# Expert products as three narrow products into one accumulator, values in one pass

## The chip, the cores and the metric

The kernel runs on one core of a Trainium2 chip. The metric is device time of one launch in microseconds (us). Engines are named as in the profile: PE is TensorE (PEld its weight loads), DVE is VectorE, ACT is ScalarE, POOL is GpSimd, SP is SyncE, which here only issues DMAs.

## The reference

One inference step of a transformer layer for 256 prompt tokens and 32 sample tokens, 288 in all, with 2048 columns each, in fp32. Cut to what matters:

```python
qkv   = x @ w_in                                   # differential attention, memory attention
x1    = layer_norm(ALPHA * x + mixed @ w_o)
q     = x1 @ peer_w_q                              # 8 heads x 2 keys x 128
s     = einsum('thcd,hcnd->thcn', q, sub_keys)     # product keys: 16 best of 128 x 128 experts per head
act   = einsum('td,tkd->tk', x1, u_tab[experts])   # 128 experts per token, 16384 in all
h     = gelu(act) * gates
y     = layer_norm(ALPHA * x1 + einsum('tk,tkd->td', h, v_tab[experts]))
```

The change concerns the last lines: the activations `act` and the values `y`.

## The kernel before

The tokens are split. For 224 "dense" tokens (`ND`) the kernel computes the activations of all 16,384 experts and masks them with the gates (zero where an expert was not chosen), so both expert tables are read once from HBM in order and are multiplied on TensorE. For the other 64 tokens the rows of the chosen experts are gathered by indirect DMAs on POOL's queue and are multiplied on VectorE.

fp32 accuracy comes from splitting: every number is hi + lo, each part in the 12 bits that one pass of TensorE carries (type fp32r). A product of weights w and data x is hi(w) hi(x) + hi(w) lo(x) + lo(w) hi(x).

**The stream.** `plan` lists all large loads in order, in units of 128 x 1024 numbers (512 KB). `stream`, `load_next` and `take` (lines 149 to 204) run it: SP's queue loads a unit into a ring of four `raw` tiles (L191), ScalarE casts it to `hi` (L165), VectorE subtracts to get `lo` (L181), and `hi` and `lo` are rings of three. `take` returns a unit's parts and at the same time issues the split of the unit two ahead and the load of the one four ahead. `tick` advances work that stands beside the stream by one stage. The order of all instructions is as written by hand; each engine works through its own queue in order.

**Activations** (lines 1031 to 1073). For each of 128 blocks of 128 experts two units of `peer_u`, transposed, give 16 steps, one for each contraction tile of 128. The moving data `ux` hold the hi part of 224 tokens and behind it their lo part, 448 columns. A step is one product of 448 columns (weights hi, L1039) and one of 224 columns (weights lo, L1041), which adds into the accumulator's first 224 columns. An accumulator is one PSUM bank. When a block is done, `finish_act` has ScalarE copy the second 224 columns into `small` (L992), multiplies them with an identity matrix into the first 224 columns (L994) and applies the gelu a stage later. In the second half of the blocks, one-hot products for the gates (L1019, four in a unit) stand in between.

**Values** (lines 1078 to 1272). The weights are the rows of `peer_v`, 128 experts x 1024 columns in a unit, and the moving data are h, hi and lo side by side, split in batches of four blocks (`batch`, L75 and L76). Eight accumulators of 448 columns fill the eight PSUM banks, so the 2048 output columns take two passes over the 128 expert blocks, one for each half of the columns, and h is split in both. A step is one 128 x 128 tile of weights: L1200 (448 columns) and L1202 (224 columns). At the end of a pass `evac` again copies the second half on ScalarE (L1117), adds it through the identity matrix (L1119), and VectorE adds the accumulator to the residual in `yT` (L1120). In the last units `turn` transposes the finished columns for the norm behind it (L1190). The gathered tokens' value rows (L948, L1111) are paced by the unit's number.

Each product on TensorE is issued with its own weight load. This is the step as the activation stage has it:

```python
nc.tensor.matmul(ps[:, :2 * ND], wh, ux[:, d].rearrange("p a t -> p (a t)"), start=(d == 0), stop=False, ...)
nc.tensor.matmul(ps[:, :ND], wl, ux[:, d, 0], start=False, stop=False, skip_group_check=True)
```

The projections of the earlier stages (`mm_tile`, L232 to L234) have three products of 256 or 288 columns for the same sum.

Of the kernel before, what the change touches and what calls it, by code (L numbers as in the profile page):

```python
# [10 lines left out]
F32R = mybir.dt.float32r  # L11
# [6 lines left out]
P = 128  # L18
D = 2048
DT = 16  # L20
# [17 lines left out]
LAG = 1  # L38
XCOLS = 928
# [10 lines left out]
def tile_stream_step(ctx: ExitStack, tc, xT_d, xn_d, memT_d, ckT_d, cv_d, cmkT_d, cmv_d,  # L50
# [22 lines left out]
    def split_to(hi, lo, raw):  # L73
        """raw = hi + lo exactly, each part in the 12 bits that one pass of the tensor engine carries"""
        nc.scalar.copy(hi, raw)  # L75
        nc.vector.tensor_sub(lo, raw, hi.bitcast(F32))  # L76

    # x1 rows of the gathered tokens, and the expert choices
# [26 lines left out]
    # ------------------------------------------------ the stream of everything large  # L105
# [38 lines left out]
    plan += [weight(v_d[i * P:(i + 1) * P, half * 1024:(half + 1) * 1024]) for half in range(2) for i in range(NKEY)]  # L144
# [4 lines left out]
    def stream(n, ahead=AHEAD):  # L149
        """splits up to the weights that are ahead units after unit n, and loads beyond them"""  # L150
# [26 lines left out]
    def settle():  # L177
        """the small parts that are due"""
        while pending:
            _, hi, lo, raw = pending.pop(0)  # L180
            nc.vector.tensor_sub(lo, raw, hi.bitcast(F32))  # L181
# [24 lines left out]
    # ------------------------------------------------ work beside the stream  # L206
    stages = []          # each advances by one stage per tick
    slow = deque()       # one at a time, by its cost on the vector engine
# [20 lines left out]
    def mm_tile(ps, part, k, d, mh, ml, n):  # L229
        """out^T [128 columns, n tokens] += one contraction tile of weights' (mh + ml)"""  # L230
        wh, wl = (w[:, k * P:(k + 1) * P] for w in part)
        nc.tensor.matmul(ps[:, :n], wh, mh[:, d, :n], start=(d == 0), stop=False)  # L232
        nc.tensor.matmul(ps[:, :n], wh, ml[:, d, :n], start=False, stop=False)  # L233
        nc.tensor.matmul(ps[:, :n], wl, mh[:, d, :n], start=False, stop=(d == DT - 1))  # L234

    def mm_unit(ps, half, mh, ml, n, ticks=(3, 7), tiles=8):
        """the next unit's contraction tiles"""
# [6 lines left out]
    def keep_warm(n):  # L244
        """products into a bank that nobody reads, so that the tensor engine's clock stays up over a pause"""
# [10 lines left out]
    def rsqrt(pool, out, v, n, rows=P):  # L256
        """out = (v + eps) ** -0.5, with a Newton step behind the square root's table"""
# [9 lines left out]
    # ------------------------------------------------ constants, memory projections  # L267
# [24 lines left out]
    def bias_job():  # L292
        """the relative bias of all heads, laid out by diagonals through DRAM"""
# [35 lines left out]
    # ------------------------------------------------ mixers  # L329
# [45 lines left out]
    def diff_attend(h, qT, kT, vT, ck, cv):  # L375
# [51 lines left out]
        def weights(t):  # L427
            # w * s0 = e0 - lam * s0 / s1 * e1
# [155 lines left out]
    # ------------------------------------------------ output projection, first norm  # L584
# [27 lines left out]
    def residual(c, ps):  # L612
        """the tokens' rows again, added to the residual"""
# [48 lines left out]
    # ------------------------------------------------ expert choice  # L662
    ROWS = (P, 96, P)

    def topk(units):
        """the 16 best experts of heads for the tokens of their tiles: scores, and both halves of their numbers;
        the units' steps take turns"""
# [89 lines left out]
    def dense_choice(t):  # L757
        """the choices of a dense token tile, its heads' units done"""
# [26 lines left out]
    def rows_job():  # L785
        """x1 rows of the gathered tokens"""
# [8 lines left out]
    def copy_job():  # L795
        """the dense tokens' part of x1, both parts side by side"""
# [13 lines left out]
    def normed_turn(c):  # L810
        """a tile of the normed rows, transposed"""
# [103 lines left out]
    # the last scores, before the units of the experts  # L915
# [8 lines left out]
    # ------------------------------------------------ experts: activations and gates  # L924
# [12 lines left out]
    class Rows:  # L937
        """half rows of the gathered tokens' experts, fetched ahead of their use"""
# [27 lines left out]
    def one_hots(t0):  # L966
        """of two tokens: the second key's choices, and the gates at the first key's"""
# [10 lines left out]
    def gate_in(t0, ps, done):  # L978
        """gates of four tokens for all experts: into h where the activation is there, aside elsewhere"""
# [9 lines left out]
    def finish_act(i, ps, gated):  # L989
        """the smaller products onto the others, and the activation; h where the gates are there"""  # L990
        small = tmpp.tile([P, ND], F32R, tag="small", name=f"small{i}")
        nc.scalar.copy(small, ps[:, ND:2 * ND])  # L992
        yield
        nc.tensor.matmul(ps[:, :ND], identr, small, start=False, stop=True, skip_group_check=True)  # L994
# [36 lines left out]
    for i in range(NKEY):  # L1031
        ps = pa()
        for half in range(2):
            n = 2 * i + half
            hi, lo = take()
            for k in range(8):
                d = half * 8 + k
                wh, wl = hi[:, k * P:(k + 1) * P], lo[:, k * P:(k + 1) * P]
                nc.tensor.matmul(ps[:, :2 * ND], wh, ux[:, d].rearrange("p a t -> p (a t)"), start=(d == 0), stop=False,  # L1039
                                 skip_group_check=True)  # L1040
                nc.tensor.matmul(ps[:, :ND], wl, ux[:, d, 0], start=False, stop=False, skip_group_check=True)  # L1041
# [36 lines left out]
    # ------------------------------------------------ experts: values  # L1078
# [4 lines left out]
    def batch(b, pieces=((0, 4),)):  # L1083
        if b < 64:
            i = 4 * (b % 32)
# [27 lines left out]
    def evac(half, dt, acc):  # L1113
        """the smaller products onto the others, and the sum onto the residual"""
        d = half * 8 + dt
        small = tmpp.tile([P, ND], F32R, tag="small", name=f"vsm{d}")
        nc.scalar.copy(small, acc[:, ND:2 * ND])  # L1117
        yield
        nc.tensor.matmul(acc[:, :ND], identr, small, start=False, stop=True, skip_group_check=True)  # L1119
        nc.vector.scalar_tensor_tensor(yT[:, d], yT[:, d], ALPHA, acc[:, :ND], op0=OP.mult, op1=OP.add)  # L1120
# [16 lines left out]
    def finish_gathered():  # L1137
        """the gathered tokens' halves together, their second norm, out"""
# [32 lines left out]
        # the rows of the dense tokens' norm, into what is free now  # L1171
# [13 lines left out]
    def turn(g, t):  # L1185
        """rows of a quarter of the columns again, in a free bank"""
# [8 lines left out]
    EARLY = {3: [(0, 0)], 4: [(1, 0), (0, 1)], 5: [(1, 1)], 6: [(2, 0)]}  # L1195
    def products(half, dt, part, i):
        """columns of the values (hi + lo) . a block's h, whole and remainder"""
        hb = batches[(half * NKEY + i) // 4][:, i % 4] if half or i else h0
        wh, wl = (w[:, dt * P:(dt + 1) * P] for w in part)
        nc.tensor.matmul(accs[dt][:, :2 * ND], wh, hb.rearrange("p a t -> p (a t)"), start=(i == 0), stop=False,  # L1200
                         skip_group_check=True)
        nc.tensor.matmul(accs[dt][:, :ND], wl, hb[:, 0], start=False, stop=False, skip_group_check=True)  # L1202

    evs, accs = [], []

    def finish(half, dt):
        """a finished accumulator's evacuation, begun; the one before it, ended"""
        g = evac(half, dt, accs[dt])
        next(g)
        if dt:  # L1210
            drain(evs.pop())
        evs.append(g)
        if half == 1:
            for g, t in EARLY.get(dt, ()):
                turn(g, t)
                quarter_stats(g, t)

    for half in range(2):
        tail = 2 + half
        groups = [[i] for i in range(NKEY - tail)] + [list(range(NKEY - tail, NKEY))]  # L1220
        for group in groups:
            last_group = len(group) > 1
            units = []
            for q, i in enumerate(group):
                units.append(take(AHEAD - q))
            if last_group and half == 1:
                while slow:
                    drain(slow.popleft())
            if group[0] == 0:
                accs[:] = [None] * 8  # L1230
            for dt in range(8):
                if group[0] == 0:
                    if half and dt == 2:
                        drain(evs.pop())
                    if not half and dt in (2, 4):
                        tick()
                    accs[dt] = pb() if dt < 4 else pa()
                for j, (part, i) in enumerate(zip(units, group)):
                    if j < 2:
                        products(half, dt, part, i)  # L1240
                    elif dt >= LAG:
                        products(half, dt - LAG, part, i)
                if len(group) == 2:
                    finish(half, dt)
                elif len(group) == 3 and dt >= LAG:
                    finish(half, dt - LAG)
            if len(group) == 3:
                for dt in range(8 - LAG, 8):
                    products(half, dt, units[2], group[2])
                    finish(half, dt)  # L1250
            if last_group and half == 1:
                turn(2, 1)
                drain(evs.pop())
                for t in range(2):
                    turn(3, t)
            n = half * NKEY + group[-1]
# [136 lines left out]
```

## Time and profile before

| | |
|---|---|
| median of 3 runs | 2013.01 us (2010.47 to 2014.66) |
| profiled execution, span | 2008.1 us (the profile gives no other time for it; 4.9 us under the median) |
| PE busy | 1983.6 us (99%), 13178 products |
| PEld busy | 1872.5 us (93%), 13178 loads |
| DVE busy | 1567.3 us (78%) |
| ACT busy | 1160.7 us (58%) |
| POOL busy | 480.9 us (24%) |
| DMA | 521.21 MB, mean 260 GB/s |
| mean granted TensorE clock | 0.997 |

The activation stage takes the span from 624.6 to about 1336 us, the value stage from there to about 1990 us. In the profile a product's duration includes its way through the array, and the ends are modelled, so neighbouring products overlap in it; the distance between two starts is what a product costs in a stream.

### The profile page before, as it was taken

To read this page: it belongs to the slowest core of one execution; us is meant where nothing else is said; L and a number is where in the kernel's file an instruction comes from. 1 tells how busy PE (TensorE), PEld (TensorE's weight loads), DVE (VectorE), ACT (ScalarE), POOL (GpSimd) and SP (SyncE) were. 2 spreads that over 40 slices of the span, in tenths; PEclk is the share of its full clock that TensorE was granted. 3 is DMA by queue.
4 is the path that set the end of the run, shared out by engine and by line. 5 is a ranking of instruction groups with operands and counts; after the bars stand their busy time and mean duration, and the time that the engine had idled before them with its cause. 6 is when DMAs were issued, how large, how long until landed. Compare 5 with 4: busy or idle time off the path is not lost.

```text
span 2008.1 us, 34989 instructions
## 1 busy us (share of the span) xinstructions
PE 1983.6 (99%) x13178; PEld 1872.5 (93%) x13178; DVE 1567.3 (78%) x2683; ACT 1160.7 (58%) x1919; POOL 480.9 (24%) x348
## 2 busy tenths in 40 slices
PE   9999999999999999999999999999999999999996
PEld 7999999999999999999999999999999999999996
DVE  5455555556788889998899999978888888888886
ACT  5345545544534555555999999854455555444553
POOL 0110000010000112222333333324443343334412
PEclk9999999999999999999999999999999999999998
DMA  8854555484445788888888888889999998999985
GB/s 294 258 165 141 153 155 153 129 287 137 154 148 162 241 291 280 277 282 283 294 298 296 293 298 302 300 288 318 335 322 343 327 333 314 323 328 321 327 264 167
DMA packets 147625, 521.21 MB, mean 260 GB/s; under 512 B 16848, under 2 KB 21088, under 8 KB 147328
## 3 DMA queue, kind: packets, MB, share of 16 engines
q1 hardware_dynamic: 103504, 360.49, 54.8%
q0 software_dynamic: 43952, 158.48, 22.0%
q8 instruction: 104, 1.70, 0.3%
q14 instruction: 65, 0.53, 0.1%
HBM read 508.33 MB, written 10.06 MB: 258 GB/s over the span
## 4 chain that ended last, share of the span: by engine, by line
PE 96%; DMA 1%; DVE 1%; ACT 1%; POOL 0%; issue 0%; SPq 0%; POOLq 0%; ACTq 0%; DVEq 0%
PE pa L1039 22%; PE pa L1200 11%; PE pb L1200 11%; PE pa L1041 11%; PE pa L232 8%; PE pa L233 7%; PE pa L234 7%; PE pb L1202 5%; PE pa L1202 5%; PE pb L1019 3%; DMA raw<-in_wmk 1%; PE pa L994 1%; PE pb L397 0%; DVE lo L181 0%; PE pa L893 0%; PE pa L319 0%
## 5 line engine op out<-in xcount | busy, mean ns | idle before, releaser
L181 DVE TENSOR_TENSOR lo<-raw,hi 128x1024 fp32r<-128x1024 f32 (+1 forms) x679 | 820.8, 1211 | 367.1 <-ACT hi L165 356.7
L165 ACT CAST hi<-raw 128x1024 fp32r<-128x1024 f32 (+1 forms) x679 | 705.5, 1040 | 497.2 <-PE pa L1200 253.8
L1039 PE MATMUL pa<-ux,hi 128*128 128x448 f32 x2048 | 669.8, 379 | 0.0
L1041 PE MATMUL pa<-ux,lo 128*128 128x224 f32 x2048 | 543.6, 265 | 0.0
L1039 PEld LDWEIGHTS pa<-ux,hi 128*128 128x128 f32 x2048 | 385.4, 188 | 29.4 <-issue 0.2
L1041 PEld LDWEIGHTS pa<-ux,lo 128*128 128x128 f32 x2048 | 391.7, 191 | 0.0
L948 POOL DMA_INDIRECT ur<-in_u,gidx x128 | 197.9, 1546 | 700.2 <-DVE ur L963 329.8
L1200 PE MATMUL pa<-hs,hi 128*128 128x448 f32 x1020 | 338.3, 376 | 0.0
L1200 PE MATMUL pb<-hs,hi 128*128 128x448 f32 x1020 | 338.0, 376 | 0.0
L948 POOL DMA_INDIRECT vr<-in_v,gidx x128 | 221.4, 1730 | 354.7 <-DVE x1g L1111 321.2
L1202 PE MATMUL pb<-hs,lo 128*128 128x224 f32 x1020 | 271.1, 266 | 0.3 <-DVE lo L181 0.3
L1202 PE MATMUL pa<-hs,lo 128*128 128x224 f32 x1020 | 271.0, 266 | 0.0
L1200 PEld LDWEIGHTS pb<-hs,hi 128*128 128x128 f32 x1020 | 191.4, 188 | 17.5
L1200 PEld LDWEIGHTS pa<-hs,hi 128*128 128x128 f32 x1020 | 191.4, 188 | 17.4
L1202 PEld LDWEIGHTS pb<-hs,lo 128*128 128x128 f32 x1020 | 195.1, 191 | 0.5 <-DVE lo L181 0.5
L232 PE MATMUL pa<-xh,hi 128*128 128x288 f32 x640 | 195.2, 305 | 0.0
L1202 PEld LDWEIGHTS pa<-hs,lo 128*128 128x128 f32 x1020 | 195.1, 191 | 0.0
L233 PE MATMUL pa<-xl,hi 128*128 128x288 f32 x640 | 188.9, 295 | 0.0
L234 PE MATMUL pa<-xh,lo 128*128 128x288 f32 x640 | 188.2, 294 | 0.0
L1111 DVE SCALAR_TENSOR_TENSOR x1g<-vr,ggate,x1g 128x1024 f32<-128x1024 f32 x128 | 163.7, 1279 | 0.0
L963 DVE SCALAR_TENSOR_TENSOR ur<-ur,x1g 128x1024 f32<-128x1024 f32 x128 | 155.7, 1216 | 0.0
L232 PEld LDWEIGHTS pa<-xh,hi 128*128 128x128 f32 x640 | 120.0, 188 | 4.9 <-issue 3.7
(346 smaller groups left out, 2706.7 us busy)
## 6 DMA issues: line engine op xcount, KB each, us to landing
raw<-in_ut SPq DMA_DIRECT2D x256, 512.0 KB, 4.4
raw<-in_v SPq DMA_DIRECT2D x255, 512.0 KB, 6.5
raw<-in_win SPq DMA_DIRECT2D x80, 512.0 KB, 3.7
raw<-in_wq SPq DMA_DIRECT2D x32, 512.0 KB, 3.6
raw<-in_wo SPq DMA_DIRECT2D x29, 512.0 KB, 3.7
raw<-in_wmv SPq DMA_DIRECT2D x8, 512.0 KB, 5.3
raw<-in_wmk SPq DMA_DIRECT2D x6, 512.0 KB, 5.8
xn<-in_xn POOLq DMA_DIRECT2D x8, 384.0 KB, 9.7
```

The source lines that it names most:

```text
L165: nc.scalar.copy(hi[:, cs], raw[:, cs])
L181: nc.vector.tensor_sub(lo, raw, hi.bitcast(F32))
L232: nc.tensor.matmul(ps[:, :n], wh, mh[:, d, :n], start=(d == 0), stop=False)
L233: nc.tensor.matmul(ps[:, :n], wh, ml[:, d, :n], start=False, stop=False)
L234: nc.tensor.matmul(ps[:, :n], wl, mh[:, d, :n], start=False, stop=(d == DT - 1))
L948: nc.gpsimd.indirect_dma_start(out=t, out_offset=None, in_=self.table, in_offset=bass.IndirectOffsetOnAxis(ap=gidx[:, a, s:s + 1], axis=0))
L963: nc.vector.scalar_tensor_tensor(rows, rows, 1.0, x1g[:, a * 1024:(a + 1) * 1024], op0=OP.mult, op1=OP.mult, accum_out=gact[:, a, s:s + 1])
L1039: nc.tensor.matmul(ps[:, :2 * ND], wh, ux[:, d].rearrange("p a t -> p (a t)"), start=(d == 0), stop=False, skip_group_check=True)
L1041: nc.tensor.matmul(ps[:, :ND], wl, ux[:, d, 0], start=False, stop=False, skip_group_check=True)
L1111: nc.vector.scalar_tensor_tensor(va, rows, ggate[:, s:s + 1], va, op0=OP.mult, op1=OP.add)
L1200: nc.tensor.matmul(accs[dt][:, :2 * ND], wh, hb.rearrange("p a t -> p (a t)"), start=(i == 0), stop=False, skip_group_check=True)
L1202: nc.tensor.matmul(accs[dt][:, :ND], wl, hb[:, 0], start=False, stop=False, skip_group_check=True)
```

## The change

A step has three products of 224 columns, all into the same 224 columns: hi(w) hi(x), hi(w) lo(x), lo(w) hi(x). The copies to `small`, the identity products and their stages in `finish_act` and `evac` are gone. In the value stage an accumulator now has 224 columns, two of them share a PSUM bank (`place`), and 16 accumulators hold all 2048 output columns, so there is one pass over the expert blocks: both column halves of a block follow each other (`V_ORDER`), h is split once (32 batches instead of 64), and all evacuations stand at the end. The last three blocks (`TAIL`) are ordered by halves, so that the first half's accumulators end early.

```diff
+    V_ORDER = [(i, half) for i in range(NKEY - TAIL) for half in range(2)]
+    V_ORDER += [(i, half) for half in range(2) for i in range(NKEY - TAIL, NKEY)]
+    plan += [weight(v_d[i * P:(i + 1) * P, half * 1024:(half + 1) * 1024]) for i, half in V_ORDER]
...
     def finish_act(i, ps, gated):
-        small = tmpp.tile([P, ND], F32R, tag="small", name=f"small{i}")
-        nc.scalar.copy(small, ps[:, ND:2 * ND])
-        yield
-        nc.tensor.matmul(ps[:, :ND], identr, small, start=False, stop=True, skip_group_check=True)
         yield
...
-                nc.tensor.matmul(ps[:, :2 * ND], wh, ux[:, d].rearrange("p a t -> p (a t)"), start=(d == 0), stop=False,
-                                 skip_group_check=True)
-                nc.tensor.matmul(ps[:, :ND], wl, ux[:, d, 0], start=False, stop=False, skip_group_check=True)
+                nc.tensor.matmul(ps[:, :ND], wh, ux[:, d, 0], start=(d == 0), stop=False, skip_group_check=True)
+                nc.tensor.matmul(ps[:, :ND], wh, ux[:, d, 1], start=False, stop=False, skip_group_check=True)
+                nc.tensor.matmul(ps[:, :ND], wl, ux[:, d, 0], start=False, stop=(d == DT - 1), skip_group_check=True)
...
+    def evac(d, n=1):
+        bank, at_ = place(d)
+        nc.vector.scalar_tensor_tensor(yT[:, d:d + n], yT[:, d:d + n], ALPHA,
+                                       banks[bank][:, at_ * ND:(at_ + n) * ND].rearrange("p (a t) -> p a t", a=n),
+                                       op0=OP.mult, op1=OP.add)
...
+    EARLY = {1: [(0, 0)], 2: [(0, 1)], 3: [(1, 0)], 4: [(1, 1)], 5: [(2, 0)], 6: [(2, 1)]}
+    def place(d):
+        return (d // 2, d % 2) if d < 8 else (4 + d % 4, (d - 8) // 4)
+
+    def products(d, part, i):
+        bank, at_ = place(d)
+        if bank not in banks:
+            banks[bank] = pb() if bank < 4 else pa()
+            first = True
+        else:
+            first = False
+        acc = banks[bank][:, at_ * ND:(at_ + 1) * ND]
+        hb = batches[i // 4][:, i % 4] if i else h0
+        wh, wl = (w[:, d % 8 * P:(d % 8 + 1) * P] for w in part)
+        nc.tensor.matmul(acc, wh, hb[:, 0], start=first, stop=False, skip_group_check=True)
+        nc.tensor.matmul(acc, wh, hb[:, 1], start=False, stop=False, skip_group_check=True)
+        nc.tensor.matmul(acc, wl, hb[:, 0], start=False, stop=(i == NKEY - 1), skip_group_check=True)
...
+    for n, (i, half) in enumerate(V_ORDER[:-TAIL]):
+        part = take()
+        for dt in range(8):
+            if n == 0 and dt in (2, 4):
+                tick()
+            products(half * 8 + dt, part, i)
+            if i == NKEY - 1 and dt % 2:
+                evac(dt - 1, 2)
+        beside(n)
+        if half == 0 and i % 4 == 1:
+            batch(i // 4 + 1)
+        if half == 1 and i % 4 == 3:
+            del batches[i // 4]
+    units = [take(AHEAD - q) for q in range(TAIL)]
...
+    for dt in range(8 + LAG):
+        for j, i in enumerate(range(NKEY - TAIL, NKEY)):
+            at_dt = dt - LAG if j == TAIL - 1 else dt
+            if 0 <= at_dt < 8:
+                products(8 + at_dt, units[j], i)
+        if dt >= LAG:
+            evac(8 + dt - LAG)
+            for g, t in EARLY.get(dt - LAG, ()):
+                turn(g, t)
+                quarter_stats(g, t)
```

## Rows read from the trace of the kernel before

**Rows 1.** Windows: start:end, length, busy us (count) by engine, clock, DMA share, GB/s.
```profile
624.00:800.00 176.00, 176.00 (x1129) 167.06 (x1128) 154.88 (x385) 98.92 (x147) 27.99 (x19) 1.00 0.78 257
1220.00:1300.00 80.00, 80.00 (x543) 76.53 (x542) 74.94 (x143) 72.67 (x166) 29.71 (x19) 1.00 0.84 294
1400.00:1500.00 100.00, 100.00 (x633) 94.62 (x632) 84.37 (x73) 50.33 (x50) 41.08 (x26) 1.00 0.94 329
```

**Rows 2.** Part 4 of the page: the chain that ended last, by engine.
```profile
PE 96%; DMA 1%; DVE 1%; ACT 1%; POOL 0%; issue 0%; SPq 0%; POOLq 0%; ACTq 0%; DVEq 0%
```

**Rows 3.** Groups, PE, value stage: shapes xcount, busy us, mean ns, idle us.
```profile
L1202 PE MATMUL pb<-hs,lo 128*128 128x224 f32 x1020 | 271.1, 266 | 0.3 <-DVE lo L181 0.3
```

**Rows 4.** Timeline of PE: start, duration us, line; block ends in the activation stage.
```profile
703.22 0.27 PE L994 MATMUL pa<-small,identr 128*128 128x224 f32 x1
...
718.69 0.27 PE L994 MATMUL pa<-small,identr 128*128 128x224 f32 x1
```

**Rows 5.** Timeline of PE, value stage: first and last of 64 L1200.
```profile
1449.76 0.38 PE L1200 MATMUL pa<-hs,hi 128*128 128x448 f32 x1
...
1469.72 0.37 PE L1200 MATMUL pa<-hs,hi 128*128 128x448 f32 x1
```

**Rows 6.** Timeline of PE: products of 256 (first two rows) and 512 columns.
```profile
20.86 0.28 PE L232 MATMUL pa<-memh,hi 128*128 128x256 f32 x1
...
21.80 0.28 PE L234 MATMUL pa<-memh,lo 128*128 128x256 f32 x1
...
44.66 0.40 PE L318 MATMUL pa<-hi,memh 128*128 128x512 f32 x1
...
46.99 0.40 PE L319 MATMUL pa<-lo,memh 128*128 128x512 f32 x1
```

**Rows 7.** Timeline of PEld (weight loads), around an identity product.
```profile
904.32 0.19 PEld L1039 LDWEIGHTS pa<-ux,hi 128*128 128x128 f32 x1
904.43 0.19 PEld L1041 LDWEIGHTS pa<-ux,lo 128*128 128x128 f32 x1
904.64 0.19 PEld L994 LDWEIGHTS pa<-small,identr 128*128 128x128 f32 x1
904.75 0.19 PEld L1039 LDWEIGHTS pa<-ux,hi 128*128 128x128 f32 x1
904.86 0.19 PEld L1041 LDWEIGHTS pa<-ux,lo 128*128 128x128 f32 x1
```

**Rows 8.** Timeline of PEld: four one-hot loads merged, and a load behind them.
```profile
1008.91 0.52 PEld L1019 LDWEIGHTS pb<-ohA,ohB 128*128 128x128 f32 x4
...
1009.47 0.19 PEld L1041 LDWEIGHTS pa<-ux,lo 128*128 128x128 f32 x1
...
1208.89 0.52 PEld L1019 LDWEIGHTS pb<-ohA,ohB 128*128 128x128 f32 x4
...
1209.45 0.19 PEld L1041 LDWEIGHTS pa<-ux,lo 128*128 128x128 f32 x1
```

**Rows 9.** Timeline of PE at the turn between the halves of the value stage.
```profile
1664.37 0.37 PE L1200 MATMUL pb<-hs,hi 128*128 128x448 f32 x1
1665.00 0.37 PE L1202 MATMUL pb<-hs,lo 128*128 128x224 f32 x1 [0.25 <-DVE lo L181]
```

**Rows 10.** Timeline of all engines at the end of the value stage.
```profile
1989.34 0.26 PE L1202 MATMUL pa<-hs,lo 128*128 128x224 f32 x1
...
1990.51 0.39 DVE L1120 SCALAR_TENSOR_TENSOR yT<-yT,pa 128x224 f32<-128x224 f32 x1 [0.18 <-PE pa L1119]
```

**Rows 11.** Groups by line, ACT, activation stage.
```profile
L992 ACT CAST small<-pa 128x224 fp32r<-128x224 f32 x127 | 42.8, 337 | 104.2 <-PE pa L1041 104.2
```

**Rows 12.** Waits, 1400 to 1600: total us, times, longest us.
```profile
ACT hi L165 <- DMA raw<-in_v: 20.0, 14, 2.7
```

**Rows 13.** Lines L232 and L233: loads by tile, ns min/median/max, first and last start.
```profile
L232 PEld LDWEIGHTS pa<-xh,hi x640: 186/187/193, 61.2 to 373.6; 128*128 128x128 f32 x160
...
L233 PEld LDWEIGHTS pa<-xl,hi x640: 186/188/193, 61.5 to 373.8; 128*128 128x128 f32 x160
```

More of the change, by code (lines that the diff above doesn't have):

```diff
@@ L38 @@
 LAG = 1
+TAIL = 3
 XCOLS = 928
@@ L143, in tile_stream_step @@
     plan += [weight(ut_d[i, half]) for i in range(NKEY) for half in range(2)]
-    plan += [weight(v_d[i * P:(i + 1) * P, half * 1024:(half + 1) * 1024]) for half in range(2) for i in range(NKEY)]
+    V_ORDER = [(i, half) for i in range(NKEY - TAIL) for half in range(2)]
+    V_ORDER += [(i, half) for half in range(2) for i in range(NKEY - TAIL, NKEY)]
+    plan += [weight(v_d[i * P:(i + 1) * P, half * 1024:(half + 1) * 1024]) for i, half in V_ORDER]
     PIECES[len(plan) - 1] = 4
@@ L1083, in batch @@
     def batch(b, pieces=((0, 4),)):
-        if b < 64:
-            i = 4 * (b % 32)
+        if b < 32:
+            i = 4 * b
             bt, o = (bigA, i) if i < SPLIT else (bigB, i - SPLIT)
@@ L1111, in use_v @@
         nc.vector.scalar_tensor_tensor(va, rows, ggate[:, s:s + 1], va, op0=OP.mult, op1=OP.add)
[L1113 to L1120, printed above, removed]
+    def evac(d, n=1):
[3 more added lines that the diff above has]
+                                       op0=OP.mult, op1=OP.add)
     def stats(pool, rows, n):
@@ L1193, in quarter_stats @@
         nc.vector.bn_stats(vs[t][:, g], nat2[g, t][:rows2[t]])
[L1195 to L1214, printed above, removed]
+    EARLY = {1: [(0, 0)], 2: [(0, 1)], 3: [(1, 0)], 4: [(1, 1)], 5: [(2, 0)], 6: [(2, 1)]}
+    banks = {}
+    def place(d):
[13 more added lines that the diff above has]
+        nc.tensor.matmul(acc, wl, hb[:, 0], start=False, stop=(i == NKEY - 1), skip_group_check=True)
@@ new lines, in beside @@
+    def beside(n):
+        nonlocal v_from
+        if n % YSTEP == YSTEP - 1 and n // YSTEP < DT // 2:
+            ds = slice(2 * (n // YSTEP), 2 * (n // YSTEP) + 2)
+            nc.gpsimd.dma_start(yT[:, ds], x1T_s[ds].rearrange("a p b -> p a b"))
+        if n == 2:
+            slow.append(gathered_h())
+        tick()
+        if "vacc" in flags and vg.used < 128:
+            if v_from is None:
+                v_from = n
+            vg.upto(128 * (n + 1 - v_from) // (VEND - v_from))
+            if vg.used == 128:
+                slow.append(finish_gathered())
@@ new lines, in tile_stream_step @@
+    for n, (i, half) in enumerate(V_ORDER[:-TAIL]):
+        part = take()
+        for dt in range(8):
+            if n == 0 and dt in (2, 4):
+                tick()
+            products(half * 8 + dt, part, i)
[7 more added lines that the diff above has]
+    units = [take(AHEAD - q) for q in range(TAIL)]
@@ L1215, in finish @@
+    while slow:
+        drain(slow.popleft())
+    for dt in range(8 + LAG):
[6 more added lines that the diff above has]
+            for g, t in EARLY.get(dt - LAG, ()):
                 turn(g, t)
                 quarter_stats(g, t)
[L1218 to L1256, printed above, removed]
-            if n % 4 == 3:
-                del batches[n // 4]
-            if n % YSTEP == YSTEP - 1 and n // YSTEP < DT // 2:
-                ds = slice(2 * (n // YSTEP), 2 * (n // YSTEP) + 2)
-                nc.gpsimd.dma_start(yT[:, ds], x1T_s[ds].rearrange("a p b -> p a b"))
-            if n == 2:
-                slow.append(gathered_h())
-            tick()
-            if n % 4 == 1:
-                batch(n // 4 + 1)
-            if "vacc" in flags and vg.used < 128:
-                if v_from is None:
-                    v_from = n
-                vg.upto(128 * (n + 1 - v_from) // (VEND - v_from))
-                if vg.used == 128:
-                    slow.append(finish_gathered())
@@ L1273, in tile_stream_step @@
+    for t in range(2):
+        turn(3, t)
     bigs.close()
@@ L1278, in tile_stream_step @@
     nc.vector.memset(mr, 1.0)
-    for g, t in ((2, 1), (3, 0), (3, 1)):
-        quarter_stats(g, t)
+    for t in range(2):
+        quarter_stats(3, t)
     for t in range(2):
```

## The prediction

> **What bounds the kernel now.** I read the table by stage first [rows 1]: TensorE is busy for all of every stretch of the two expert stages, while VectorE reaches 84 to 94% and the DMA engines 78 to 94%. Busy time alone is weak evidence, since the ends of products are modelled, so the chain of waits comes next [rows 2]: 96% of it is TensorE, led by the lines that the change edits (L1039, L1041, L1200, L1202). Then the groups of the value stage [rows 3]: before 1020 products TensorE sat idle for 0.3 us. TensorE waits for nobody there, so the time is the number of products times the spacing of their starts. Everything below is about that spacing, read from starts, never from durations.
>
> A step is one 128x128 tile of weights (hi and lo). Today it is a wide product (448 columns, weights hi) and a narrow one (224 columns, weights lo). Block by block, the activation stage repeats every 15.47/3 = 5.157 us (four identity products, the first and the last shown in [rows 4]): 16 steps and one identity product. In the value stage 63 steps take 19.96 us, or 316.8 ns each [rows 5].
>
> What sets these 317 ns? Two limits can be read off. First, columns: where three equal products of 256 columns follow each other, eight spacings take 0.94 us, 117.5 ns each; with 512 columns ten take 2.33 us, 233 ns [rows 6]. That is 0.457 ns a column with nothing left over for the instruction itself, so 448 columns would need 205 ns and 224 columns 102.5 ns, together 307. The pair takes 10 more. Second, weight loads: every product has one, and it begins when the product before has begun. Beside a wide product it is free. Beside a narrow one it isn't: the load for L1039 begins at 904.32 and the next can't begin until 904.43; around the identity product three loads in a row stand at 904.64, 904.75, 904.86 [rows 7], about 110 ns apart although 224 columns are done in 102.5. The longest unbroken series is that of the one-hot products: from the first of four loads to the second load of the step behind them (L1041; that of L1039 lies between) are five spacings, 0.56 us both times, 112 ns each [rows 8]. So the narrow product of today's pair is already limited by the load of what follows: 316.8 - 205 = 112 ns, and in the activation stage (5.157 - 0.11)/16 = 315.4, less 205 = 110 ns. Two independent readings, chain and difference, agree on 110 to 112.
>
> **The change part by part.** *Three narrow products for a wide and a narrow one.* Columns per step stay 672, but loads go from two to three, and no product is left that is long enough to cover one. Each spacing is then the longer of 102.5 (columns) and the load. I take 111 ns, the middle of 110 to 112: 333 ns a step. Ends: 102.5 if columns alone count (307 ns); 108 if a steady series runs like the tightest pairs read before rounding to 0.11 (324 ns); 112 as in the one-hot series (336 ns). 111 is nearest to the rows that are series, not pairs.
>
> The Trainium skill, "TensorE: Matmul & The Clock Gate", section "LDWEIGHTS (loading the stationary operand)", prices a load at its columns over 1.2 GHz, 107 ns for 128. The loads here stand 110 to 112 ns apart in series, so the rule has the right limit and a few ns too little. By it a step would be 320 ns and the whole change come out near zero (worked out as a rival below).
>
> *Activation stage.* A block becomes 16 x 0.333 = 5.328 us and loses its identity product, against 5.157 with it: +0.171 us x 128 blocks = +21.9 us. (With 111 ns for the identity product inside 5.157, its removal is 14.2 us of gain, and the steps cost 36.) Four one-hot products stand in some units both before and after and cost four loads either way: no change.
>
> *Value stage.* (333 - 316.8) ns x 2048 steps = +33.2 us. Sixteen identity products go, at 0.11 us [rows 7]: -1.8 us. At today's turn from the first half of the columns to the second, one product is followed only 0.63 us later instead of 0.21 [rows 9]; with one pass there is no such turn: -0.4 us. At the end, today's last accumulator goes product, ScalarE copy, identity product, VectorE sum: 1.17 us from the start of the last L1202 to the start of L1120 [rows 10]. Afterwards VectorE reads the accumulator some 0.3 us behind the product: -0.8 us. Together -3.0 us.
>
> *Copies on ScalarE* (127 counted x 337 ns [rows 11], and 16 more): worth nothing, since TensorE waits for neither ScalarE nor VectorE. The same holds for splitting h into hi and lo 32 times instead of 64. If the cover went, which needs TensorE to become faster, this would be the relief; here TensorE becomes slower and all others gain slack.
>
> *One pass over the experts.* Both halves of an expert row block now follow each other. Each batch of h serves eight units instead of four; the next is issued behind the third of its predecessor's eight units, five units (some 13 us) ahead of need, into a ring of two whose older tile was last read three units before. The loads on SP's queue are the same 256 of 512 KB in another order; the gathered rows on POOL's queue keep their pace per unit. Today ScalarE waited 20.0 us for weights in 200 us [rows 12], without TensorE noticing; a unit that is 5% longer needs 5% less from the DMA engines. Cost zero; bound below zero none, since TensorE is not waiting; above, what a late load could cost if alternate halves landed later, at most the longest such wait, 2.7 us, now and then: some us in all.
>
> *Sixteen accumulators in eight banks.* The first unit opens banks of one pool, the second those of the other, so the start waits no more than today. All evacuations move to the end: four of double width during the last unit of the first half, then eight behind their products with one step's lag, which today's tail has as well. Nothing queued behind them is wanted by TensorE but the transposes, spread over the tail as today. Zero, within 1 us.
>
> Sum: 21.9 + 33.2 - 3.0 = +52.1 us on a span of 2008.1, 2060.2. The median of the runs, 2013.01, lies 4.9 above that span; I carry this over: 2065.
>
> **The rivals.** *Columns alone set the spacing* (other side). For it: sums of columns are unchanged, 144 identity products go, and a product may start, by its row, before its load's row ends. Against: rows 7, where 224 columns did not let the loads closer than about 110 ns. It would make a step 307 ns: 16 x 0.307 = 4.912, -0.245 x 128 = -31.4; -9.8 ns x 2048 = -20.1; -3.0: 1958. It decides if loads of a series stand under 103 ns apart. The same time would follow if the compiler gave the two products with the same hi weights one load (two loads of 111 ns are less than 307): against it, L232 and L233 use the same weights back to back today, and both have 640 loads [rows 13].
>
> By the formula of the Trainium skill, "TensorE: Matmul & The Clock Gate", section "Back-to-back issue gap" (columns over 2.4 GHz and 2.5 ns for each product) a step would gain one fixed 2.5 ns, +10 us, against 144 identity products of 96 ns: about 2008. The 512-column products here are 233 ns apart, where that formula gives 216, so I don't build on it.
>
> *The load costs less in series than it looks* (no change). Spacings shown to 10 ns leave room for 107: a step of 320 ns, activation blocks 5.12 (-4.7 us), value steps +3.2 ns (+6.6), -3.0: 2012. Against: the one-hot series, 112. At 108: 324 ns, +3.5 + 14.7 - 3.0 = +15: 2028.
>
> *The series is slower still*: 113 ns and more, for instance through the hand-over between two accumulators of one bank: 339 ns, +34.2 + 45.5 - 3.0: 2090.
>
> *VectorE or the DMA engines become the bound.* Only if TensorE gets faster: at 1220 to 1300 VectorE is 94% busy [rows 1], so a faster TensorE would get some of it back as waits. With a slower one this rival is empty; it limits the first.
>
> **How the numbers follow.** Likeliest, 110 to 112 ns: 0.70, 330 ns gives 2053 (+15.7 + 27.0 - 3.0) and 336 gives 2077, the middle 2065. About 108 ns (2028): 0.13. 113 and above (2090): 0.08. Near 107 (2012): 0.03. Columns alone or a shared load (1958, more with VectorE in the way): 0.06. The range leaves out the last two and half of the slow tail: 2026 to 2085. A measurement of this kernel can tell about 0.2% (4 us) from no change; faster holds 0.06, within it 0.03, slower 0.91.
>
> **What would show it.** Right: three loads per step about 111 ns apart in both stages, 333 ns a step, blocks of 5.33 us without one-hots, weight loads 50% more in these stages, TensorE still without idle time, VectorE's and DMA's shares down by some 5%. Wrong: product starts 103 ns apart (columns), steps of 320 to 324 (cheaper loads), one load for two products, or idle time of TensorE in the value stage released by VectorE or a DMA (another bound).

## The result, and the profile after

The changed kernel takes 2075.72 us (median of 4 runs, 2074.56 to 2076.99) against 2013.33 us in the same series: 1.031 times as long, 95% interval 1.0293 to 1.0322. The prediction was 2065 us, with a range of 2026 to 2085.

First the table by stage, for [rows 1] (columns as there). The second window lies 20 us later and the third 50, since the activation stage is longer now.

```profile
624.00:800.00 176.00, 175.51 (x1565) 174.96 (x1564) 150.96 (x387) 83.67 (x109) 23.20 (x18) 1.00 0.75 244
1240.00:1320.00 80.00, 80.00 (x719) 80.00 (x718) 71.75 (x137) 71.58 (x155) 31.33 (x18) 1.00 0.84 290
1450.00:1550.00 100.00, 100.00 (x898) 100.00 (x897) 76.58 (x65) 43.16 (x43) 28.39 (x24) 1.00 0.91 315
```

Two figures matter. The weight loads, the second busy figure, went from 95 or 96 to 99 or 100% of a stretch: there is hardly a moment without one. And VectorE's share in the value stage fell from 84 to 77%, the DMA engines' from 0.94 to 0.91: both have more slack there. The chain of waits is as one-sided as in [rows 2]:

```profile
PE 97%; DVE 1%; DMA 1%; ACT 1%; POOL 0%; issue 0%; SPq 0%; POOLq 0%; ACTq 0%; DVEq 0%
```

Now the spacing itself, on the timeline of weight loads (start us, duration us), for [rows 7]:

```profile
903.85 0.19 PEld L1039 LDWEIGHTS pa<-ux,hi 128*128 128x128 f32 x1
903.97 0.19 PEld L1040 LDWEIGHTS pa<-ux,lo 128*128 128x128 f32 x1
904.08 0.19 PEld L1038 LDWEIGHTS pa<-ux,hi 128*128 128x128 f32 x1
904.19 0.19 PEld L1039 LDWEIGHTS pa<-ux,hi 128*128 128x128 f32 x1
904.30 0.19 PEld L1040 LDWEIGHTS pa<-ux,lo 128*128 128x128 f32 x1
```

Four spacings in 0.45 us: the 0.11 that was to be seen before only behind a narrow product is now the distance of all. Over 63 steps, as in [rows 5], the first and last of 64 first products of a step (the timeline of PE, first the activation and then the value stage):

```profile
699.85 0.27 PE L1038 MATMUL pa<-ux,hi 128*128 128x224 f32 x1
...
720.96 0.27 PE L1038 MATMUL pa<-ux,hi 128*128 128x224 f32 x1
...
1449.97 0.27 PE L1210 MATMUL pa<-hs,hi 128*128 128x224 f32 x1
...
1471.08 0.27 PE L1210 MATMUL pa<-hs,hi 128*128 128x224 f32 x1
```

Both stages take 21.11 us for 63 steps: 335.1 ns a step, 111.7 ns a product, where the value stage had 316.8 ns a step before. The stages as a whole, from the timelines of PE: before, the first product of the activation stage, and the first of the value stage (its last L1202 is in [rows 10]):

```profile
624.64 0.47 PE L1039 MATMUL pa<-ux,hi 128*128 128x448 f32 x1
...
1335.98 0.37 PE L1200 MATMUL pb<-h,hi 128*128 128x448 f32 x1
```

and after, with the last product of the value stage:

```profile
628.06 0.37 PE L1038 MATMUL pa<-ux,hi 128*128 128x224 f32 x1
...
1364.88 0.28 PE L1210 MATMUL pb<-h,hi 128*128 128x224 f32 x1
...
2055.00 0.28 PE L1212 MATMUL pa<-hs,lo 128*128 128x224 f32 x1
```

So, between first products and on to the last one: activations 711.3 to 736.8 us, +25.5; values 653.4 to 690.1, +36.8; what follows 18.7 to 18.0 (spans 2008.1 and 2073.0), -0.7. Together +61.6, against +62.4 between the medians. The profiled executions differ by 64.9, because the changed one also came 3.4 us later to the activation stage. That part lies ahead of the changed instructions. Behind the first norm, where both kernels run the same ones, a window of ten us shows a granted TensorE clock of 1.00 (of full speed) before and 0.66 after. First before:

```profile
496.00:506.00 10.00, 9.84 (x60) 7.66 (x60) 9.99 (x24) 7.79 (x18) 0.00 (x0) 1.00 0.24 80
```

and after:

```profile
497.00:507.00 10.00, 9.91 (x44) 8.03 (x45) 8.19 (x19) 6.56 (x16) 0.00 (x0) 0.66 0.21 69
```

The new steps don't decide this: in the same place (496 to 506 us) the kernel with three narrow products in two passes, shown below, has 1.00, and the one with sums on GpSimd, whose steps are the old ones, 0.63.

One more thing is new. For [rows 3], the group of the value stage's last product now has 1.3 us of idle time before it, in one place (groups by line, value stage; then the timeline of PE there):

```profile
L1212 PE MATMUL pa<-hs,lo 128*128 128x224 f32 x1016 | 278.8, 274 | 1.3 <-DVE lo L184 1.3
```

```profile
2043.37 0.27 PE L1211 MATMUL pa<-hs,hi 128*128 128x224 f32 x1
2044.93 0.37 PE L1212 MATMUL pa<-hs,lo 128*128 128x224 f32 x1 [1.29 <-DVE lo L184]
```

The starts lie 1.56 us apart instead of 0.11, and TensorE waited for VectorE's lo. This is what VectorE did then, on its own timeline:

```profile
2041.11 2.63 DVE L1115 SCALAR_TENSOR_TENSOR yT<-yT,pb 128x448 f32<-128x448 f32 x4 [1.16 <-PE pb L1212]
2043.66 2.56 DVE L184 TENSOR_TENSOR lo<-raw,hi 128x1024 fp32r<-128x1024 f32 x5
```

The four double evacuations of the first half stand in VectorE's queue ahead of the lo that TensorE needs next, and they waited 1.16 us for TensorE's products themselves.

### The profile page after: what moved, and what is told of

It reads as the page before. It is cut to its first block, busy times and chain, and to the rows that moved or that the text cites. A ratio compares the mean times of both kernels' runs of the same rounds, so it can differ in the third digit from the quotient of the medians.

```text
span 2073.0 us, 42538 instructions
## 1 busy us (share of the span) xinstructions
PE 2048.9 (99%) x17130; PEld 2006.7 (97%) x17130; DVE 1545.7 (75%) x2647; ACT 1097.1 (53%) x1743; POOL 407.6 (20%) x348
## 4 chain that ended last, share of the span: by engine, by line
PE 97%; DVE 1%; DMA 1%; ACT 1%; POOL 0%; issue 0%; SPq 0%; POOLq 0%; ACTq 0%; DVEq 0%
PE pa L1040 11%; PE pa L1039 11%; PE pa L1038 11%; PE pa L235 8%; PE pa L236 7%; PE pa L237 7%; PE pa L1212 6%; PE pb L1212 6%; PE pb L1210 6%; PE pb L1211 6%; PE pa L1210 5%; PE pa L1211 5%; PE pb L1018 2%; DMA raw<-in_wmv 1%; PE pb L400 0%; PE pa L896 0%
## 5 line engine op out<-in xcount | busy, mean ns | idle before, releaser
L1038 PE MATMUL pa<-ux,hi 128*128 128x224 f32 x2048 | 569.6, 278 | 0.0
L1040 PE MATMUL pa<-ux,lo 128*128 128x224 f32 x2048 | 565.1, 276 | 0.0
L1039 PE MATMUL pa<-ux,hi 128*128 128x224 f32 x2048 | 561.9, 274 | 0.0
L1038 PEld LDWEIGHTS pa<-ux,hi 128*128 128x128 f32 x2048 | 393.2, 192 | 0.2 <-issue 0.2
L1039 PEld LDWEIGHTS pa<-ux,hi 128*128 128x128 f32 x2048 | 393.2, 192 | 0.0
L951 POOL DMA_INDIRECT ur<-in_u,gidx x128 | 190.1, 1485 | 734.8 <-DVE ur L966 427.9
L1212 PE MATMUL pa<-hs,lo 128*128 128x224 f32 x1016 | 278.8, 274 | 1.3 <-DVE lo L184 1.3
L1212 PE MATMUL pb<-hs,lo 128*128 128x224 f32 x1016 | 278.6, 274 | 0.0
L1210 PE MATMUL pa<-hs,hi 128*128 128x224 f32 x1016 | 278.3, 274 | 0.0
L1210 PE MATMUL pb<-hs,hi 128*128 128x224 f32 x1016 | 277.9, 274 | 0.0
L1211 PE MATMUL pa<-hs,hi 128*128 128x224 f32 x1016 | 277.4, 273 | 0.0
L1211 PE MATMUL pb<-hs,hi 128*128 128x224 f32 x1016 | 277.4, 273 | 0.0
L951 POOL DMA_INDIRECT vr<-in_v,gidx x128 | 155.9, 1218 | 450.9 <-DVE x1g L1110 429.4
L1210 PEld LDWEIGHTS pb<-hs,hi 128*128 128x128 f32 x1016 | 195.1, 192 | 0.0
L1211 PEld LDWEIGHTS pb<-hs,hi 128*128 128x128 f32 x1016 | 195.1, 192 | 0.0
```

Of the source, the lines that this page charges most:

```text
L951: nc.gpsimd.indirect_dma_start(out=t, out_offset=None, in_=self.table, in_offset=bass.IndirectOffsetOnAxis(ap=gidx[:, a, s:s + 1], axis=0))
L1038: nc.tensor.matmul(ps[:, :ND], wh, ux[:, d, 0], start=(d == 0), stop=False, skip_group_check=True)
L1039: nc.tensor.matmul(ps[:, :ND], wh, ux[:, d, 1], start=False, stop=False, skip_group_check=True)
L1210: nc.tensor.matmul(acc, wh, hb[:, 0], start=first, stop=False, skip_group_check=True)
L1211: nc.tensor.matmul(acc, wh, hb[:, 1], start=False, stop=False, skip_group_check=True)
L1212: nc.tensor.matmul(acc, wl, hb[:, 0], start=False, stop=(i == NKEY - 1), skip_group_check=True)
```

## The experiments

The theory: a product of 224 columns costs one weight load, 112 ns in a series, and a wide product covers the load behind it, so the change trades two loads a step, one of them free, for three that count. Its rivals: the one pass over the experts (order of the loads, two accumulators in a bank) costs the time; or columns and loads add up. A fourth, that every product has a fixed price of 112 ns whatever it loads, was not tested by a run of its own; the traces have something on it, told with the half product.

**Three narrow products in the activation stage alone.** The kernel before with

```diff
-nc.tensor.matmul(ps[:, :2 * ND], wh, ux[:, d].rearrange("p a t -> p (a t)"), ...)
-nc.tensor.matmul(ps[:, :ND], wl, ux[:, d, 0], ...)
+nc.tensor.matmul(ps[:, :ND], wh, ux[:, d, 0], ...)
+nc.tensor.matmul(ps[:, :ND], wh, ux[:, d, 1], ...)
+nc.tensor.matmul(ps[:, :ND], wl, ux[:, d, 0], ...)
```

and without the copy and identity product of `finish_act`.

> The kernel before with three narrow products in the activation stage alone; its values stay in two passes with a wide and a narrow product. Theory (a product of 224 columns costs one weight load, about 112 ns in series): activation blocks 5.37 us instead of 5.16, the stage +25 us, value steps unchanged at 317 ns: about 2038 us. Rival (the time was lost by the one pass over the experts: two accumulators in a bank, halves of rows in turn): activation stage not slower than before, 2013 us or less.

2038.8 us, 1.013 (1.0113 to 1.0147). On the timeline of PE, 64 steps of each stage, first and last start:

```profile
699.91 0.27 PE L1035 MATMUL pa<-ux,hi 128*128 128x224 f32 x1
...
721.01 0.27 PE L1035 MATMUL pa<-ux,hi 128*128 128x224 f32 x1
...
1449.65 0.38 PE L1196 MATMUL pa<-hs,hi 128*128 128x448 f32 x1
...
1469.61 0.37 PE L1196 MATMUL pb<-hs,hi 128*128 128x448 f32 x1
```

334.9 ns a step where the products are narrow and 316.8 where they aren't, in one kernel. The activation stage, in which only the products and their sum changed, takes 736.8 us, as in the changed kernel; the value stage stays at 653.5 (653.4 before). So the activations carry their 25 us by themselves, and one pass can't be the whole cause.

**Narrow products, values in two passes.** The same edit also in `products`, and `evac` reads the accumulator directly; everything else, the two passes and one accumulator in a bank included, as before.

```diff
-small = tmpp.tile([P, ND], F32R, tag="small", name=f"vsm{d}")
-nc.scalar.copy(small, acc[:, ND:2 * ND])
-nc.tensor.matmul(acc[:, :ND], identr, small, ...)
...
-nc.tensor.matmul(accs[dt][:, :2 * ND], wh, hb.rearrange("p a t -> p (a t)"), ...)
-nc.tensor.matmul(accs[dt][:, :ND], wl, hb[:, 0], ...)
+nc.tensor.matmul(accs[dt][:, :ND], wh, hb[:, 0], ...)
+nc.tensor.matmul(accs[dt][:, :ND], wh, hb[:, 1], ...)
+nc.tensor.matmul(accs[dt][:, :ND], wl, hb[:, 0], ...)
```

> The kernel before with three narrow products in both stages and no identity sums, but the values still in two passes with one accumulator in a bank. Theory (loads): value steps 336 ns as in the changed kernel, 2074 to 2078 us. Rival (one pass costs time): value steps clearly under 336 ns, 2060 us or less. Rival (one pass saves time that hides part of the loss): value steps 336 ns and a total over 2080 us.

2073.61 us, 1.0304 (1.0286 to 1.0321). The value stage, first and last of 64 steps:

```profile
1449.96 0.27 PE L1193 MATMUL pa<-hs,hi 128*128 128x224 f32 x1
...
1471.06 0.28 PE L1193 MATMUL pb<-hs,hi 128*128 128x224 f32 x1
```

334.9 ns, with one accumulator in a bank and the old order of the loads. The one pass, the sharing of banks and the order of the halves are therefore free in the steps, and bring nothing either: this kernel's profile spends 688.2 us in the value stage, the changed one 690.1, and 1.5 of the difference is the wait at the end shown above.

**Half a product.** The changed kernel with the middle product cut to 112 columns in both stages:

```diff
-nc.tensor.matmul(ps[:, :ND], wh, ux[:, d, 1], ...)
+nc.tensor.matmul(ps[:, :ND // 2], wh, ux[:, d, 1, :ND // 2], ...)
```

> The changed kernel; the product with the remainder of x or h takes 112 of its 224 columns in both stages, so the remainders of half the tokens are left out. Theory (loads): three loads a step as before the cut, spacing 112 ns though 112 columns need only 51, so 2076 us within 4. Rival (columns count): 51 ns less on each of 4096 steps, 210 us less, 1866 us.

2078.4 us (2 runs), 1.0325 (1.0304 to 1.0345): not one us less, for a sixth of the columns left out. The activation stage takes 736.8 us with them and without. The value stage of the profiled execution is 3.2 us longer than the changed kernel's; there the granted clock is 0.57 from 2044 to 2052 us. The timelines show why nothing is gained. Products, three of a step and the next:

```profile
904.16 0.27 PE L1038 MATMUL pa<-ux,hi 128*128 128x224 f32 x1
904.27 0.22 PE L1039 MATMUL pa<-ux,hi 128*128 128x112 f32 x1
904.33 0.33 PE L1040 MATMUL pa<-ux,lo 128*128 128x224 f32 x1
904.49 0.27 PE L1038 MATMUL pa<-ux,hi 128*128 128x224 f32 x1
```

and the loads:

```profile
904.17 0.19 PEld L1039 LDWEIGHTS pa<-ux,hi 128*128 128x128 f32 x1
904.28 0.19 PEld L1040 LDWEIGHTS pa<-ux,lo 128*128 128x128 f32 x1
904.39 0.19 PEld L1038 LDWEIGHTS pa<-ux,hi 128*128 128x128 f32 x1
904.50 0.19 PEld L1039 LDWEIGHTS pa<-ux,hi 128*128 128x128 f32 x1
```

The short product's successor is recorded 0.06 us behind it, but it gives the time back: the one after that comes 0.16 us later. The loads keep their 0.11 whatever the products do.

On the rival of a fixed price per product, the 0.06 us say that two products may start closer together than 0.11. And where the kernel before loads fewer columns of weights, loads stand closer too (timeline of PEld, pairs of the scores, L834 with 64 columns of weights and L832 with 128):

```profile
522.26 0.19 PEld L834 LDWEIGHTS pb<-keys,qT 128*64 128x64 f32 x2
522.62 0.30 PEld L832 LDWEIGHTS pb<-keys,qT 128*128 128x128 f32 x2 [0.17 <-issue]
```

One such load lasts 0.134 and 0.188 us by itself, so the second starts 0.06 us behind the first with 64 columns, 0.11 with 128. These are pairs and not series; a series of narrow products with smaller loads stands in no run.

**256 columns.** The changed kernel; in the activation stage each product takes 32 more columns, whose results nobody reads:

```diff
+n2 = 256 if d < DT - 1 else ND
-nc.tensor.matmul(ps[:, :ND], wh, ux[:, d, 0], ...)
+nc.tensor.matmul(ps[:, :256], wh, uxf[:, c:c + 256], ...)
-nc.tensor.matmul(ps[:, :ND], wh, ux[:, d, 1], ...)
+nc.tensor.matmul(ps[:, :n2], wh, uxf[:, c + ND:c + ND + n2], ...)
-nc.tensor.matmul(ps[:, :ND], wl, ux[:, d, 0], ...)
+nc.tensor.matmul(ps[:, :256], wl, uxf[:, c:c + 256], ...)
```

> The changed kernel; in the activation stage each product takes 256 columns instead of 224, the extra 32 go to columns of the accumulator that nobody reads. Theory (the longer of load and columns): 117.5 ns a product instead of 112, 5.5 x 6144 = +34 us, 2110 us, steps of 352 ns. Rival (columns add to a load): 32 columns x 0.457 ns x 6144 = +90 us, 2166 us. Rival (neither, a fixed price per product): 2076 us.

2115.37 us (2 runs), 40 us over the changed kernel. 64 steps on the timeline of PE:

```profile
699.92 0.28 PE L1041 MATMUL pa<-ux,hi 128*128 128x256 f32 x1
...
722.15 0.28 PE L1041 MATMUL pa<-ux,hi 128*128 128x256 f32 x1
```

352.9 ns a step, 117.6 ns a product: columns (256 x 0.457 = 117) have overtaken the load. The stage grew by 37 us, to 774.0; the theory gave 34, added columns would have given 90. Together with the run before: a middle product of 112 or of 224 columns makes no difference, at 256 the price is the columns'. It is the longer of the two, not their sum.

**No sums.** The kernel before without the copies to `small` and the 144 identity products, so the smaller products are left out.

```diff
-small = tmpp.tile([P, ND], F32R, tag="small", name=f"small{i}")
-nc.scalar.copy(small, ps[:, ND:2 * ND])
-nc.tensor.matmul(ps[:, :ND], identr, small, ...)
...
-small = tmpp.tile([P, ND], F32R, tag="small", name=f"vsm{d}")
-nc.scalar.copy(small, acc[:, ND:2 * ND])
-nc.tensor.matmul(acc[:, :ND], identr, small, ...)
```

> The kernel before without its copies and identity products: the smaller products are left out of the sums (144 narrow products fewer, everything else as before). Theory (a narrow product behind a narrow one costs one load): 144 x 0.11 = 16 us less, and some 0.4 us at the turn between the halves and 0.6 at the end: 1996 us. Rival (the identity product only fills time in which the next load runs, so it is free): 2013 us.

1994.57 us, 0.9908 (0.9893 to 0.9923): 19 us less. In the profiles the activation stage lost 14.9 us (128 products: 116 ns each), the value stage 2.6. The identity products were worth what the prediction took them for; the change got that back and paid more.

**The sums elsewhere.** If the identity products cost 16 us and the wide products are worth keeping, another engine can do the sum. In the first 63 activation blocks, on VectorE:

```diff
+if i < G0 - 1:
+    both = tmpp.tile([P, ND], F32, tag="tmp", name=f"both{i}")
+    nc.vector.tensor_add(both, ps[:, :ND], small.bitcast(F32))
+    yield
+    nc.scalar.activation(hrow(i), both, AF.Gelu)
+    return
 nc.tensor.matmul(ps[:, :ND], identr, small, start=False, stop=True, skip_group_check=True)
```

> The kernel before; in the first 63 activation blocks VectorE adds the copied smaller products (0.39 us each) in place of the identity product, all else as before. Theory: 63 x 0.11 = 7 us less, 2006 us, if VectorE (89% busy there, 96% with this) keeps ahead of TensorE. Rival (VectorE gets late with lo): TensorE waits for it, and the time is 2013 us or more.

2008.52 us, 0.9981 (0.9971 to 0.9991), the only version with all products in its sums that beats both kernels, by some 4 us (2 to 6) of the 7 expected. Its profile shows the activation stage 5.7 us shorter, and TensorE waiting for lo for the first time there (groups by line, 640 to 960 us):

```profile
L1047 PE MATMUL pa<-ux,lo 128*128 128x224 f32 x1006 | 267.3, 266 | 0.9 <-DVE lo L181 0.9
```

VectorE is 95% busy in that stretch, so part of the gain goes to waits; the rest of the difference lies within the interval.

The same on GpSimd, with ScalarE copying both halves:

```diff
+if i < G0 - 1:
+    both = tmpp.tile([P, ND], F32, tag="tmp", name=f"both{i}")
+    nc.scalar.copy(both, ps[:, :ND])
+    yield
+    nc.gpsimd.tensor_tensor(out=both, in0=both, in1=small.bitcast(F32), op=OP.add)
+    yield
+    yield
+    nc.scalar.activation(hrow(i), both, AF.Gelu)
+    return
```

> The kernel before; in the first 63 activation blocks ScalarE copies both halves and GpSimd adds them in place of the identity product. Theory: 7 us less, 2006 us, with VectorE's load unchanged. Rival (GpSimd's sums delay the gathers on its queue, and the gathers VectorE): less than 3 us gained, or a loss.

2025.13 us, 1.0056 (1.0041 to 1.007): a loss. Groups by line, then waits (total us, times, longest), 640 to 960 us:

```profile
L997 POOL TENSOR_TENSOR both<-both,small 128x224 f32<-128x224 f32 x60 | 87.2, 1454 | 60.7 <-ACT both L995 59.9
...
L1050 PE MATMUL pa<-ux,lo 128*128 128x224 f32 x957 | 257.6, 269 | 10.4 <-DVE lo L181 10.1
```

```profile
ACT bigA L1000 <- POOL both L997: 70.8, 28, 5.0
```

The sum takes 1.45 us there, against 0.38 on VectorE, and the gelu that waits for it holds ScalarE up to 5.0 us at a time, with the next hi cast queued behind it. So hi, then lo, then TensorE are late. The rival had the right sign, and this is a way that it did not name. Its own way, late gathers, shows once (groups by line, same stretch; this idle time is 0.0 in the kernel before):

```profile
L963 DVE SCALAR_TENSOR_TENSOR ur<-ur,x1g 128x1024 f32<-128x1024 f32 x37 | 45.0, 1218 | 4.6 <-DMA ur<-in_u,gidx 4.6
```

Until 698.7 us VectorE waited for gathered rows. TensorE then waited 3.2 us for lo, and from 701 to 706 us its granted clock was 0.50. The run doesn't split the loss between the two ways, nor show why these rows came late.

**The order at the end.** The changed kernel with lo ahead of the evacuations:

```diff
-            if i == NKEY - 1 and dt % 2:
+            if i == NKEY - 1 and dt in (1, 3):
+                settle()
                 evac(dt - 1, 2)
...
     units = [take(AHEAD - q) for q in range(TAIL)]
+    for dt in (5, 7):
+        evac(dt - 1, 2)
```

> The changed kernel; at the end of the values' first half, lo of the unit that waits goes to VectorE ahead of the double evacuations, and two of these four go behind lo of the last unit. Theory (the wait of 1.5 us before the last units is VectorE's order): the gap of 1.56 us between two products goes, 1 to 2 us less than the changed kernel, 2074 us. Rival (the last weights come late by themselves): the gap stays, 2076 us.

2075.33 us (2 runs) against 2075.72 for the changed kernel, no difference that two runs could show. The trace shows it: VectorE's order is now lo, two evacuations, lo, two evacuations,

```profile
2042.01 1.23 DVE L184 TENSOR_TENSOR lo<-raw,hi 128x1024 fp32r<-128x1024 f32 x1 [1.45 <-ACT hi L168]
2043.15 1.15 DVE L1115 SCALAR_TENSOR_TENSOR yT<-yT,pb 128x448 f32<-128x448 f32 x2
2044.22 1.43 DVE L184 TENSOR_TENSOR lo<-raw,hi 128x256 fp32r<-128x256 f32 x4
2045.56 1.14 DVE L1115 SCALAR_TENSOR_TENSOR yT<-yT,pb 128x448 f32<-128x448 f32 x2
```

no two products there start more than 0.19 us apart, and the value stage takes 688.6 instead of 690.1 us.

## Why the prediction was right or wrong

**Right: the bound and the mechanism.** TensorE is the only bound, spacings of starts decide, and a product of 224 columns costs a load. Shown by runs is that its price of 112 ns doesn't come from columns: cutting them changed nothing, adding them cost what the longer of two limits gives (37 us for 34), and the activation stage alone paid its share. That the other limit is the load is read from the traces: the loads are what stays 0.11 us apart, and loads of 64 columns of weights stand 0.06 apart. The rival of columns alone (1958 us) is out by 118 us; a shared load, with the same time, is out too, for the trace has three a step.

**Mis-sized: the load, 111 ns, measured 111.7.** The prediction took the middle of its two readings; the one-hot series [rows 8], 112, was the better one, because it alone was an unbroken series. That it serves is in part luck: the one-hot products are not of hi and lo but of plain fp32 (two records for each call), whose columns are dearer, 216 ns between starts for the 256 columns of L461. Their 128 columns alone would ask for 108 of the 112 ns. 335.1 instead of 333 ns is 4.3 us in each stage: the activations came to +25.5 for the +21.9 predicted, 0.7 us less than with that correction, which is not traced.

**Wrong: evacuations at the end "zero, within 1 us".** The text said that nothing behind them is wanted by TensorE but the transposes. The lo of the last units is, on VectorE's queue, and it cost 1.5 us; the last experiment took it away. With 4.3 us from the load this explains the value stage, +36.8 for the +31.0 predicted (33.2 less 1.8 and 0.4).

**Right: the small terms.** The tail behind the last product is 0.7 us shorter for the 0.8 predicted; the copies, the halved splitting of h and the order of the loads moved nothing (narrow products in two passes: the same steps). The identity products, priced at 0.11 us, measured 0.116 in the activation stage.

The stages thus came to 9.5 us more than forecast: 8.6 are the load's 0.7 ns too little and 1.5 the queue, less the 0.7 of the activations. The measured median lies 10.7 us over the forecast. There the 3.4 us ahead of the activation stage come in, and against them that the median is now 2.7 us over the profiled span, where 4.9 had been carried over.

The Trainium skill, "TensorE: Matmul & The Clock Gate", section "LDWEIGHTS (loading the stationary operand)", prices this load at its columns over 1.2 GHz, 107 ns. The series in these runs stands at 111.6 to 111.7 in every kernel with narrow products: the rule names the limit, and a sum made with it ends near no change, 64 us off. The formula by which the prediction reckons 2008 us is given by the Trainium skill, same page, section "Back-to-back issue gap", for a product by itself and not for a stream of loads and products, so that time says nothing about this kernel.

## What to carry to other kernels

Count weight loads as well as columns: here a product costs the longer of its columns (0.457 ns each for hi and lo) and the next load (112 ns). By an estimate from these two numbers, 112/0.457, fewer columns buy nothing under about 245; measured are 112, 224 and 256. One wide product (448 columns, some 205 ns) is cheaper than two narrow ones of the same sum (223 ns). Read such a price from an unbroken series in the trace and from starts; a pair that hides one load shows only half of it. When work is moved to the end of a stage, look at what stands behind it in the queue of the engine that does it, not only at who waits for its result.

## What the runs showed of the hardware that was not expected

A short product can be recorded as followed after 0.06 us, without any gain: the next one is 0.16 us away, and only the loads, 0.11 us apart throughout, show the true rate. The weights are loaded anew even when two products in a row use the same ones, which the prediction had read from L232 and L233: L1038 and L1039 have 2048 loads each.

A wait of TensorE can be followed by a lower clock. Behind the 3.2 us in the run with sums on GpSimd the granted clock was 0.50 from 701 to 706 us, its lower level, and a step took 0.59 us instead of 0.31. Behind the 1.56 us between two products at the end of the values it fell in the profiled execution with half a product (0.57 from 2044 to 2052 us), and in that of the changed kernel it didn't.
